# Block products of the feed-forward parts add onto values put into PSUM by ScalarE and VectorE, with one PSUM bank kept for them

## The chip, the cores and the metric

The kernel runs on one core of one Trainium2 chip. The metric is the device time of a run in microseconds (us). The engines are TensorE (PE; its weight loads are shown as PEld), VectorE (DVE), ScalarE (ACT), GpSimd (POOL) and SyncE (SP). PSUM holds what TensorE writes: eight banks, each 128 partitions by 512 float32 values.

## The reference

A causal decoder trunk of two layers on 512 tokens of width 1024 in float32. Layer 0 mixes tokens by dilated attention, layer 1 by causal pooling. A SwiGLU feed-forward part of width 2816 follows each mixer, and this is where the change lies:

```python
def swiglu_ffn(h, w_gate_up, w_down):
    gu = h @ w_gate_up
    gate, up = gu[..., :D_FF], gu[..., D_FF:]
    return (jax.nn.silu(gate) * up) @ w_down

for i in range(DEPTH):
    ...
    x = x + swiglu_ffn(rmsnorm(x, ffn_norm[i]), w_ffn_gate_up[i], w_ffn_down[i])
return rmsnorm(x, final_norm)
```

## The kernel before

Activations lie transposed: chunk `X[k]` holds 128 features by 512 tokens, eight chunks. A float32 operand is split into a rounded part `hi` and a rest `lo` (`split`: one ScalarE copy, L93, and one VectorE subtraction, L96), and a product of two operands takes three matmuls for each chunk of 128: hi·hi, hi·lo, lo·hi.

There are two kinds of products. A plain one (`Product`, L328 to L331) has 512 columns and takes a bank from `ps()`, a pool of eight rotating banks. A block product follows Strassen's scheme with Winograd's sums: two output chunks by two halves of the tokens make a 2 by 2 block matrix, and seven products of 256 columns (`mult`, L461 to L463) replace eight. Each has 4 chunks, so 12 matmuls. `w_pair` and `w_dblock` are the weights for it; `Pair` loads them and forms their sums (L192, L193) and splits, one step at each `pump()`. The sums of the activations are made by `prepare` (for gate and up) and by `operands`, `operands_right` and `operands_left` (for down).

`chained` is the block product of the feed-forward parts. It runs the products "11", "1", "2", "21", "3", "22", "4" in this order, which is also TensorE's order. Three accumulators are used: `alpha` takes "11", and then "2", "3" and "4" on top; ScalarE copies its state to `a`, `b` and `c` ahead of each addition (L537, L545, L553). `gamma` takes "1" (copied to `d`, L541), and "22" on top. `beta` takes "21". VectorE then forms the quarters: `beta + a` (L549), `b - gamma` (L558), `d - c` (L554), and the fourth is the negative of `alpha`.

`strassen_pair` uses `chained` for gate and up of one hidden chunk: two quarters are the gate, which goes through Silu (L1202) and is multiplied onto the other two (L1203, L1204). Each layer has 18 such pairs (chunks 4 to 21; chunks 0 to 3 take plain products). For the down projection hidden chunks 2 to 9 and 10 to 17 form two blocks of four `chained` products each, whose quarters are added to `X` by `down` (L1234). Hidden chunks 0, 1 and 18 to 21 take plain products. Over both layers that is 36 pairs and 16 down blocks, 52 block products.

What the engines do is ordered by a scheduler in the language's layer from the program's order and its priorities. Each engine then runs its own queue in order, and waits on semaphores: counts of what another engine or queue has finished.

Between attention and the first feed-forward part stands `residual(KC - 1, f.p)`: VectorE adds the last attention output product into `X[7]` (L1064). Right behind it `lead = begin(2, 1, range(KC - 1))` starts two plain products of the feed-forward part on the first seven chunks, while the last chunk's scaling and squares are still under way (`note`, L392, L393, L381, L383).

Of the kernel before, what the change touches and what calls it, by code (L numbers as in the profile page):

```python
# [15 lines left out]
P = 128  # L16
# [48 lines left out]
def trunk(ctx: ExitStack, tc: tile.TileContext, xT, xN, norms, w_first, w_qk, w_qkp, w_v0p, w_v12, w_out, w_outp, w_pair, w_down, w_dblock, w_pin, w_pgrp,  # L65
# [16 lines left out]
    def ps():  # L82
        return psum.tile([P, S], F32, tag="ps", name="ps")

# [7 lines left out]
    def split(hi, lo, v, pin=False):  # L92
# [3 lines left out]
        nc.vector.tensor_tensor(lo, v, hi.bitcast(F32), op=OP.subtract)  # L96

    def split_neg(hi, lo, v):
        nc.scalar.activation(hi, v, AF.Copy, scale=-1.0)
        nc.vector.scalar_tensor_tensor(lo, v, -1.0, hi.bitcast(F32), op0=OP.mult, op1=OP.subtract)  # L100

# [198 lines left out]
    class Product:  # L300


        def __init__(self, n, ins, w=None, keep=None):
            self.n, self.ins, self.done, self.p, self.w = n, ins, 0, ps(), w
            self.sizes = units_of(n)
            self.tiles, self.keep = keep or [], keep is not None
# [64 lines left out]
    def stream(layer):  # L371
        return lambda k: operand[layer, k]
# [59 lines left out]

    def begin(n, layer, ks):
        return [Product(KC, stream(layer)).add(ks) for i in range(n)]

# [84 lines left out]

    def chained(T, one, two, scratch, n, inner=False, after={}):
# [12 lines left out]

        wb = part(unit, "b")
        mult(alpha, wb, 0, T, "11", n)
        nc.scalar.copy(a, alpha)  # L537
# [7 lines left out]
        nc.scalar.copy(b, alpha)  # L545
        behind(2)
        mult(beta, wb, 1, T, "21", n)
        wb.done()
        nc.vector.tensor_add(one[:, left], beta, a)  # L549
# [8 lines left out]
        nc.vector.tensor_sub(one[:, right], b, gamma)  # L558
        behind(5)
        w = part(unit, "l")  # L560
        mult(alpha, w, 0, T, "4", n, on=True)
        w.done()
        if not inner:
            nc.scalar.activation(two[:, left], alpha, AF.Copy, scale=-1.0)
        behind(6)
        return alpha

# [37 lines left out]
    with tc.tile_pool(name="opool", bufs=1) as opool:  # L605
        with tc.tile_pool(name="apool", bufs=1) as apool:
# [473 lines left out]
            residual(KC - 1, f.p)  # L1080

    with tc.tile_pool(name="fpool", bufs=2) as fpool:

# [12 lines left out]
        def ffn(layer, nxt, lead, row):  # L1096
# [21 lines left out]
            def prepare(k):  # L1118
# [37 lines left out]
            def operands_right(i, v):  # L1156
                u, t = U["u"], U["t"]
                nc.vector.tensor_sub(t[:, H2:], t[:, :H2], v[:, H2:])
# [6 lines left out]
                nc.vector.tensor_sub(u[:, :H2], v[:, H2:], u[:, H2:])  # L1165
                split(*B["3", i], u[:, :H2])
# [7 lines left out]
            def later(f, *a):  # L1174
                return lambda: f(*a)
# [7 lines left out]

            def strassen_pair(u, first=None, right=None):
# [5 lines left out]
                def act_right():  # L1190
                    nc.scalar.activation(gt[:, H2:], gt[:, H2:], AF.Silu)
                    nc.vector.tensor_mul(u[:, H2:], u[:, H2:], gt[:, H2:])
                    right()

                if first:
                    hooks.setdefault(2, []).extend([later(give, ("t", k, 1)) for k in range(K2)] + [first])
                if right:
                    hooks.setdefault(3, []).append(lambda: nc.scalar.activation(gt[:, :H2], gt[:, :H2], AF.Silu))
                    hooks.setdefault(5, []).append(act_right)
                left = chained(T, gt, u, ftile, K2, inner=True, after=hooks)  # L1200
                if not right:
                    nc.scalar.activation(gt, gt, AF.Silu)  # L1202
                    nc.vector.tensor_mul(u[:, H2:], u[:, H2:], gt[:, H2:])  # L1203
                nc.vector.scalar_tensor_tensor(u[:, :H2], left, -1.0, gt[:, :H2], op0=OP.mult, op1=OP.mult)  # L1204

            def gate_up(j, ahead):
# [3 lines left out]
                if j < NPLAIN:  # L1210
                    plain_pair(j, u)
                elif block and odd and j == FC - 1:
                    strassen_pair(u, later(operands, i, U["even"]), later(operands_right, i, u))
                else:
                    strassen_pair(u)
# [10 lines left out]
                elif not odd:  # L1226
                    U["even"] = u
                elif j == FC - 1:
                    operands_left(i, u)
                else:  # L1230
                    late.extend([later(operands, i, U["even"]), later(operands_right, i, u), later(operands_left, i, u)])
# [7 lines left out]
            for first, end, block in PARTS:  # L1239
# [32 lines left out]

        lead = begin(2, 1, range(KC - 1))
        row = finish(lead, 1, [KC - 1])
# [260 lines left out]
```

## Time and profile before

| what | value |
| --- | --- |
| median of 3 runs | 1184.02 us (1183.59 to 1184.98) |
| profiled execution | 1185.19 us |
| its span, first to last instruction | 1183.4 us |
| mean granted clock of TensorE | 0.999 |
| PE, DVE, ACT, POOL busy | 1173.5, 992.7, 750.4, 174.1 us |

Each row of instructions gives the line, the engine, the operation, the tile written and the tiles read, and a count; then the busy time, the mean duration in ns, and the idle time of the engine just before, with what ended it. `L549` is line 549 of the kernel before, unless the text says that it is one of the changed kernel. `ps` is any PSUM tile of the rotating pool, `near` and `far` hold split operands, `w` and `half` split weights, `raw` loaded weights. A timeline row gives the start, the duration and the instruction.

### The profile page before, as it was taken

What the parts mean: (1) busy time and instruction counts of PE and PEld (TensorE: products, weight loads), DVE (VectorE), ACT (ScalarE), POOL (GpSimd) and SP (SyncE); (2) the same over time, 40 slices, a digit from 0 to 9 for tenths busy, and PEclk for the clock granted to TensorE, in tenths of its full rate; (3) what the DMA queues carried; (4) which work ended last, traced back from release to release, by engine and by line L of the source; (5) the groups of instructions that cost most, each with busy time, mean ns of one, the idle gap of its engine ahead of it and who ended that gap; (6) DMA issues with size and microseconds to landing.
All of it is one profiled execution on the core that took longest, in us unless ns stands there. A gap on an engine that the chain in (4) does not pass through costs nothing.

```text
span 1183.4 us, 25574 instructions
## 1 busy us (share of the span) xinstructions
PE 1173.5 (99%) x10182; PEld 1122.6 (95%) x10182; DVE 992.7 (84%) x1747; ACT 750.4 (63%) x1341; POOL 174.1 (15%) x169
## 2 busy tenths in 40 slices
PE   9999999999999999999999999999999999999997
PEld 7899999999999989889999999988889999999997
DVE  8987898889789988799988988657789988898875
ACT  8764664656556666757756766776575776676553
POOL 2111111211011002301111111112030111111100
PEclk9999999999999999999999999999999999999999
DMA  8757666665766557957777787798595777777732
GB/s 288 166 125 196 166 164 159 172 156 149 187 159 158 153 159 203 244 109 196 192 194 199 190 202 191 201 260 204 117 203 121 190 199 194 191 196 195 188 90 73
DMA packets 85017, 209.97 MB, mean 177 GB/s; under 512 B 7952, under 2 KB 13216, under 8 KB 84896
## 3 DMA queue, kind: packets, MB, share of 16 engines
q1 hardware_dynamic: 53104, 145.63, 37.3%
q0 software_dynamic: 31504, 62.41, 32.6%
q8 instruction: 80, 1.31, 0.4%
q14 instruction: 41, 0.34, 0.1%
q10 hardware_dynamic: 288, 0.29, 0.1%
HBM read 206.19 MB, written 2.10 MB: 176 GB/s over the span
## 4 chain that ended last, share of the span: by engine, by line
PE 97%; issue 1%; ACT 1%; DVE 1%; POOL 0%; DVEq 0%; POOLq 0%; ACTq 0%
PE ps L461 21%; PE ps L463 21%; PE ps L462 21%; PE ps L328 7%; PE ps L331 7%; PE ps L329 7%; PE ps L637 2%; PE ps L852 2%; PE ps L638 2%; PE ps L639 2%; PE ps L943 2%; PE ps L730 1%; PE ps L749 1%; ACT w L93 0%; PE ps L914 0%
## 5 line engine op out<-in xcount | busy, mean ns | idle before, releaser
L93 ACT ACTIVATE w<-raw 128x1024 fp32r<-128x1024 f32 x271 | 286.5, 1062 | 150.3 <-PE ps L463 78.8
L96 DVE TENSOR_TENSOR w<-raw,w 128x1024 fp32r<-128x1024 f32 x271 | 330.6, 1223 | 47.7 <-ACT w L93 43.4
L461 PE MATMUL ps<-far,w 128*128 128x256 f32 x896 | 246.5, 275 | 0.0
L462 PE MATMUL ps<-far,w 128*128 128x256 f32 x896 | 246.5, 275 | 0.0
L463 PE MATMUL ps<-far,w 128*128 128x256 f32 x896 | 246.4, 275 | 0.0
L461 PE MATMUL ps<-near,w 128*128 128x256 f32 x749 | 210.9, 282 | 0.0
L463 PE MATMUL ps<-near,w 128*128 128x256 f32 x749 | 207.1, 276 | 0.0
L462 PE MATMUL ps<-near,w 128*128 128x256 f32 x749 | 207.0, 276 | 0.0
L462 PEld LDWEIGHTS ps<-far,w 128*128 128x128 f32 x896 | 168.2, 188 | 0.1
L461 PEld LDWEIGHTS ps<-far,w 128*128 128x128 f32 x896 | 168.2, 188 | 0.1
L463 PEld LDWEIGHTS ps<-far,w 128*128 128x128 f32 x896 | 168.2, 188 | 0.0
L461 PEld LDWEIGHTS ps<-near,w 128*128 128x128 f32 x749 | 140.7, 188 | 0.5
L462 PEld LDWEIGHTS ps<-near,w 128*128 128x128 f32 x749 | 140.8, 188 | 0.0
L463 PEld LDWEIGHTS ps<-near,w 128*128 128x128 f32 x749 | 140.8, 188 | 0.0
L328 PE MATMUL ps<-near,w 128*128 128x512 f32 (+1 forms) x332 | 125.9, 380 | 0.0
L331 PE MATMUL ps<-near,w 128*128 128x512 f32 (+1 forms) x332 | 125.0, 376 | 0.0
L329 PE MATMUL ps<-near,w 128*128 128x512 f32 (+1 forms) x332 | 124.9, 376 | 0.0
L176 POOL DMA_DIRECT2D raw<-w_pair x36 | 43.6, 1210 | 297.0 <-DMA raw<-w_pair 123.7
L331 PEld LDWEIGHTS ps<-near,w 128*128 128x128 f32 x332 | 62.3, 188 | 11.6
L328 PEld LDWEIGHTS ps<-near,w 128*128 128x128 f32 x332 | 62.3, 188 | 11.5 <-ACT near L93 0.4
L329 PEld LDWEIGHTS ps<-near,w 128*128 128x128 f32 x332 | 62.5, 188 | 11.3 <-DVE near L96 0.2
L192 DVE TENSOR_TENSOR raw<-raw 128x512 f32<-128x512 f32 x87 | 59.7, 686 | 11.5 <-issue 9.7
(342 smaller groups left out, 2730.3 us busy)
## 6 DMA issues: line engine op xcount, KB each, us to landing
raw<-w_pair SPq DMA_DIRECT2D x80, 512.0 KB, 5.1
raw<-w_qkp SPq DMA_DIRECT2D x42, 512.0 KB, 4.6
raw<-w_pair POOLq DMA_DIRECT2D x36, 512.0 KB, 7.6
raw<-w_dblock SPq DMA_DIRECT2D x32, 512.0 KB, 4.5
raw<-w_qkp POOLq DMA_DIRECT2D x21, 512.0 KB, 7.9
rawhalf<-w_pair SPq DMA_DIRECT2D x36, 256.0 KB, 5.3
raw<-w_v SPq DMA_DIRECT2D x16, 512.0 KB, 4.2
raw<-w_dblock POOLq DMA_DIRECT2D x16, 512.0 KB, 7.3
```

The costliest lines, as they stand in the source:

```text
L93: made = nc.scalar.activation(hi, v, AF.Copy)
L96: nc.vector.tensor_tensor(lo, v, hi.bitcast(F32), op=OP.subtract)
L176: nc.gpsimd.dma_start(self.b.rearrange("p (a c) -> p a c", a=2), self.src[:, None, 3 * n:].to_broadcast([P, 2, n]), accum_op=OP.add)
L192: nc.vector.tensor_add(a[:, :n], a[:, :n], b[:, :n])
L328: nc.tensor.matmul(self.p[:, cols], w[0][:, s], mh[:, cols], start=self.done == 0, stop=False)
L329: nc.tensor.matmul(self.p[:, cols], w[0][:, s], ml[:, cols], start=False, stop=False)
L331: nc.tensor.matmul(self.p[:, cols], w[1][:, s], mh[:, cols], start=False, stop=self.done == self.n)
L461: nc.tensor.matmul(dst, w.t[0][:, c], th, start=k == 0 and not on, stop=False, skip_group_check=on)
L462: nc.tensor.matmul(dst, w.t[0][:, c], tl, start=False, stop=False, skip_group_check=on)
L463: nc.tensor.matmul(dst, w.t[1][:, c], th, start=False, stop=k == n - 1, skip_group_check=on)
L637: nc.tensor.matmul(o, mh, wh, start=k == 0, stop=False)
L638: nc.tensor.matmul(o, mh, wl, start=False, stop=False)
```

## The change

The three quarters that VectorE formed after the products are formed by the accumulation in PSUM. After "11" ScalarE writes the copy of alpha into `beta` instead of into `a`, and "21" adds onto it. After "2" VectorE writes `b - d` into `gamma`, and "22", whose operand is no longer negated, adds onto that. The first quarter is then read from `beta`, the third from `gamma`. `split_neg` becomes `split`.

`beta` has a fixed bank of its own, `seeded`. The pool of eight banks is closed after attention, and a pool of seven and the kept bank are opened; the first lead product of layer 0 also goes into the kept bank.

In `strassen_pair` Silu becomes two calls of 256 columns that read `beta` and `gamma` in PSUM. In the down blocks `X[m]` takes two adds of 256 columns from PSUM instead of one of 512 from `one`. The branches that are taken out (`first`, `right`, the deferred `down`) never ran with this kernel's table `PARTS`, whose last part is no block.

```diff
-    psum = ctx.enter_context(tc.tile_pool(name="psum", bufs=8, space=PSUM))
+    first_banks = ExitStack()
+    banks = [first_banks.enter_context(tc.tile_pool(name="psum", bufs=8, space=PSUM))]
...
     def ps():
-        return psum.tile([P, S], F32, tag="ps", name="ps")
+        return banks[-1].tile([P, S], F32, tag="ps", name="ps")
...
-    def begin(n, layer, ks):
-        return [Product(KC, stream(layer)).add(ks) for i in range(n)]
+    def begin(n, layer, ks, p=None):
+        return [Product(KC, stream(layer), p=None if i else p).add(ks) for i in range(n)]
...
-        alpha, beta, gamma = (ps()[:, :H2] for i in range(3))
-        ab, cd = scratch("first"), scratch("sums")
-        a, b, c, d = ab[:, left], ab[:, right], cd[:, left], cd[:, right]
+        alpha, gamma = (ps()[:, :H2] for i in range(2))
+        beta = seeded[0][:, :H2]
+        bs, cd = scratch("first"), scratch("sums")
+        b, c, d = bs[:, left], cd[:, left], cd[:, right]
...
         mult(alpha, wb, 0, T, "11", n)
-        nc.scalar.copy(a, alpha)
+        nc.scalar.copy(beta, alpha)
...
         nc.scalar.copy(b, alpha)
+        nc.vector.tensor_sub(gamma, b, d)
         behind(2)
-        mult(beta, wb, 1, T, "21", n)
+        mult(beta, wb, 1, T, "21", n, on=True)
         wb.done()
-        nc.vector.tensor_add(one[:, left], beta, a)
...
         mult(gamma, wm, 1, T, "22", n, on=True)
         wm.done()
-        nc.vector.tensor_sub(one[:, right], b, gamma)
...
-        return alpha
+        return beta, gamma, alpha
...
+    first_banks.close()
+    banks.append(ctx.enter_context(tc.tile_pool(name="psum7", bufs=7, space=PSUM)))
+    seeded = [ctx.enter_context(tc.tile_pool(name="seeded", bufs=1, space=PSUM)).tile([P, S], F32, tag="seeded", name="seeded")]
...
-                split_neg(*n, b22)
+                split(*n, b22)
...
-                split_neg(*B["22", i], v[:, H2:])
+                split(*B["22", i], v[:, H2:])
...
-                left = chained(T, gt, u, ftile, K2, inner=True, after=hooks)
-                if not right:
-                    nc.scalar.activation(gt, gt, AF.Silu)
-                    nc.vector.tensor_mul(u[:, H2:], u[:, H2:], gt[:, H2:])
+                beta, gamma, left = chained(T, u, ftile, K2, inner=True, after=hooks)
+                nc.scalar.activation(gt[:, :H2], beta, AF.Silu)
+                nc.scalar.activation(gt[:, H2:], gamma, AF.Silu)
+                nc.vector.tensor_mul(u[:, H2:], u[:, H2:], gt[:, H2:])
...
-                        one, two = ftile("one"), ftile("two")
-                        chained(D, one, two, ftile, (end - first) // 2, after=waiting())
-                        for q, v in ((m, one), (m + 1, two)):
-                            if last and m < KC - 2:
-                                late.append(later(down, q, v, last))
-                            else:
-                                down(q, v, last)
+                        two = ftile("two")
+                        parts = chained(D, two, ftile, (end - first) // 2, after=waiting())
+                        for a, p in enumerate(parts[:2]):
+                            x = X[m][:, a * H2:(a + 1) * H2]
+                            nc.vector.tensor_add(x, x, p)
+                        down(m + 1, two, last)
...
-        lead = begin(2, 1, range(KC - 1))
+        lead = begin(2, 1, range(KC - 1), seeded[0])
```

How the order of instructions moves is shown at three places. In each pair of blocks the first is the kernel before and the second the changed one, with its own line numbers. TensorE at the first lead product of layer 0, with the semaphores that each matmul waits for (`DVE_49` counts VectorE's work, `Activation_49` ScalarE's, `DMASW3_49` a DMA queue):

```order
L331 MATMUL ps<-near,w 128x512
L328 MATMUL ps<-near,w 128x512 [waits Activation_49]
L329 MATMUL ps<-near,w 128x512
L331 MATMUL ps<-near,w 128x512 [waits DMASW3_49]
L328 MATMUL ps<-near,w 128x512
```

```order
L328 MATMUL ps<-near,w 128x512
L325 MATMUL seeded<-near,w 128x512 [waits DVE_49,Activation_49]
L326 MATMUL seeded<-near,w 128x512
L328 MATMUL seeded<-near,w 128x512 [waits DMASW3_49]
L325 MATMUL seeded<-near,w 128x512
```

The first lead product (`seeded<-near,w`) waits for VectorE as well; the count in the built program is that of the residual add L1064 of `X[7]` (L1061 of the changed kernel).

VectorE in a gate/up pair of layer 1 in which operands of the down projection are also made (the pair that starts at 940.8 us; `gt` is the gate, `first` and `sums` hold `a` to `d`):

```order
L1165 TENSOR_TENSOR u<-u 128x256
L96 TENSOR_TENSOR near<-t,near 128x256
L96 TENSOR_TENSOR near<-u,near 128x256 x2
L1171 SCALAR_TENSOR_TENSOR u<-t,u 128x256
L549 TENSOR_TENSOR gt<-ps,first 128x256
L96 TENSOR_TENSOR w<-raw,w 128x1024
L554 TENSOR_TENSOR u<-sums 128x256
L96 TENSOR_TENSOR near<-u,near 128x256
L96 TENSOR_TENSOR w<-raw,w 128x1024
L558 TENSOR_TENSOR gt<-first,ps 128x256
```

```order
L1166 TENSOR_TENSOR u<-u 128x256
L97 TENSOR_TENSOR near<-t,near 128x256
L97 TENSOR_TENSOR near<-u,near 128x256
L544 TENSOR_TENSOR ps<-first,sums 128x256
L97 TENSOR_TENSOR near<-u,near 128x256
L1172 SCALAR_TENSOR_TENSOR u<-t,u 128x256
L97 TENSOR_TENSOR w<-raw,w 128x1024
L552 TENSOR_TENSOR u<-sums 128x256
L97 TENSOR_TENSOR near<-u,near 128x256
L97 TENSOR_TENSOR w<-raw,w 128x1024 x2
```

L549 and L558 are gone, and the seed of gamma (L544) stands two operand instructions ahead of where L549 stood.

ScalarE in the same pair (`sums<-ps` is `d` or `c`, `first<-ps` is `a` or `b`):

```order
L545 COPY first<-ps 128x256
L93 ACTIVATE near<-u 128x256
L93 ACTIVATE w<-raw 128x1024
L93 ACTIVATE near<-u 128x256
L553 COPY sums<-ps 128x256
L93 ACTIVATE w<-raw 128x1024 x2
L93 ACTIVATE half<-rawhalf 128x512
L1202 ACTIVATE gt<-gt 128x512
L537 COPY first<-ps 128x256
```

```order
L543 COPY first<-ps 128x256
L94 ACTIVATE near<-u 128x256
L94 ACTIVATE w<-raw 128x1024
L94 ACTIVATE near<-u 128x256
L1191 ACTIVATE gt<-seeded 128x256
L551 COPY sums<-ps 128x256
L94 ACTIVATE w<-raw 128x1024 x2
L1192 ACTIVATE gt<-ps 128x256
L94 ACTIVATE half<-rawhalf 128x512
L535 COPY seeded<-ps 128x256
```

The first half of Silu (L1191) moves ahead of the copy of `c`, the second (L1192) behind the two weight splits; the copy that made `a` now writes `seeded`. In the down blocks VectorE's add of `beta` into `X` stands right behind the seed of gamma.

More of the change, by code (lines that the diff above doesn't have):

```diff
@@ L300, in trunk, with __init__ @@
     class Product:
[L303 to L304 removed]
+        def __init__(self, n, ins, w=None, keep=None, p=None):
+            self.n, self.ins, self.done, self.p, self.w = n, ins, 0, ps() if p is None else p, w
             self.sizes = units_of(n)
@@ L519, in seven, with chained @@
         behind(6)
-    def chained(T, one, two, scratch, n, inner=False, after={}):
+    def chained(T, two, scratch, n, inner=False, after={}):
         (unit,), = units.popleft()
         left, right = slice(0, H2), slice(H2, S)
-        alpha, beta, gamma = (ps()[:, :H2] for i in range(3))
-        ab, cd = scratch("first"), scratch("sums")
-        a, b, c, d = ab[:, left], ab[:, right], cd[:, left], cd[:, right]
+        alpha, gamma = (ps()[:, :H2] for i in range(2))
+        beta = seeded[0][:, :H2]
+        bs, cd = scratch("first"), scratch("sums")
+        b, c, d = bs[:, left], cd[:, left], cd[:, right]
         def behind(i):
@@ L1182, in waiting, with strassen_pair @@
                 return hooks
-            def strassen_pair(u, first=None, right=None):
+            def strassen_pair(u):
                 gt = ftile("gt")
@@ L1188, in strassen_pair @@
                     hooks.setdefault(1, []).append(later(keep, *U.pop("keep")))
-                def act_right():
-                    nc.scalar.activation(gt[:, H2:], gt[:, H2:], AF.Silu)
-                    nc.vector.tensor_mul(u[:, H2:], u[:, H2:], gt[:, H2:])
[L1193 to L1199, printed above, removed]
-                left = chained(T, gt, u, ftile, K2, inner=True, after=hooks)
-                if not right:
-                    nc.scalar.activation(gt, gt, AF.Silu)
-                    nc.vector.tensor_mul(u[:, H2:], u[:, H2:], gt[:, H2:])
+                beta, gamma, left = chained(T, u, ftile, K2, inner=True, after=hooks)
+                nc.scalar.activation(gt[:, :H2], beta, AF.Silu)
+                nc.scalar.activation(gt[:, H2:], gamma, AF.Silu)
+                nc.vector.tensor_mul(u[:, H2:], u[:, H2:], gt[:, H2:])
                 nc.vector.scalar_tensor_tensor(u[:, :H2], left, -1.0, gt[:, :H2], op0=OP.mult, op1=OP.mult)
@@ L1211, in gate_up @@
                     plain_pair(j, u)
-                elif block and odd and j == FC - 1:
-                    strassen_pair(u, later(operands, i, U["even"]), later(operands_right, i, u))
                 else:
```

5 lines of the change are left out of this document (removed).

## Prediction

> **What bounds the kernel now.** I read the page's busy times and chain first, then the waits of TensorE alone, then stretches of the feed-forward parts, then single instructions at the places that the change touches. From the page, busy time and the head of the chain that ended last:
>
> ```profile
> PE 1173.5 (99%) x10182; PEld 1122.6 (95%) x10182; DVE 992.7 (84%) x1747; ACT 750.4 (63%) x1341; POOL 174.1 (15%) x169
> ...
> PE 97%; issue 1%; ACT 1%; DVE 1%; POOL 0%; DVEq 0%; POOLq 0%; ACTq 0%
> ```
>
> TensorE (PE) is 97% of the chain. Its spans are modelled, so I ask what it waited for, and count its matmuls in four stretches that hold block products (us, busy and count of each engine, granted clock, DMA):
>
> ```profile
> PE ps L914 <- DVE idle L911: 1.2, 1, 1.2
> PE ps L780 <- PE ps L463: 0.5, 1, 0.5
> PE ps L780 <- DVE far L768: 0.3, 1, 0.3
> ...
> 521.00:616.00 95.00, 95.00 (x840) 95.00 (x839) 84.11 (x148) 64.59 (x112) 11.01 (x10) 1.00 0.70 182
> 616.00:759.00 143.00, 143.00 (x1265) 143.00 (x1264) 124.87 (x211) 94.98 (x167) 16.84 (x14) 1.00 0.74 190
> 902.00:998.00 96.00, 96.00 (x845) 95.88 (x844) 85.12 (x150) 65.10 (x113) 11.52 (x10) 1.00 0.71 181
> 998.00:1150.00 152.00, 152.00 (x1343) 152.00 (x1342) 131.04 (x219) 99.89 (x173) 16.34 (x14) 1.00 0.69 178
> ```
>
> TensorE's waits come to 2.0 us in all, and all lie before the feed-forward parts (L911, L768 and L780 are attention code). In the stretches one matmul of 256 columns starts every 113 ns: 95/840 = 0.1131, 143/1265 = 0.1130, 96/845 = 0.1136, 152/1343 = 0.1132. VectorE (DVE) is busy for 86 to 89% of them and nothing of that reaches TensorE. So a product of 12 matmuls takes 1.36 us, and a block product of seven 9.5 us. The change leaves these counts alone: it can gain only what TensorE waits for, which here is nothing, and it can lose wherever it makes TensorE wait.
>
> **The change part by part.** First what it takes off VectorE and ScalarE (ACT). Groups by line and shape (count | busy us, mean ns | idle before):
>
> ```profile
> L549 DVE TENSOR_TENSOR gt<-ps,first 128x256 f32<-128x256 f32 x36 | 15.2, 422 | 10.2 <-PE ps L463 10.2
> L558 DVE TENSOR_TENSOR gt<-first,ps 128x256 f32<-128x256 f32 x36 | 15.0, 415 | 0.1
> L516 DVE TENSOR_TENSOR ps<-ps,sums 128x512 f32<-128x512 f32 x21 | 14.6, 693 | 0.0
> L1234 DVE TENSOR_TENSOR x<-x,two 128x512 f32<-128x512 f32 x16 | 11.0, 686 | 0.0
> L1234 DVE TENSOR_TENSOR x<-x,one 128x512 f32<-128x512 f32 x16 | 11.0, 686 | 0.0
> L537 ACT COPY first<-ps 128x256 f32<-128x256 f32 x52 | 19.4, 373 | 14.9 <-PE ps L463 14.7
> L564 ACT ACTIVATE two<-ps 128x256 f32<-128x256 f32 x16 | 6.2, 385 | 4.2 <-PE ps L463 4.2
> L93 ACT ACTIVATE near<-u 128x256 fp32r<-128x256 f32 x48 | 19.9, 415 | 8.0 <-DVE u L1204 6.9 <-DVE u L1165 0.6 <-DVE u L1171 0.5
> L1202 ACT ACTIVATE gt<-gt 128x512 f32<-128x512 f32 x36 | 22.2, 618 | 2.2 <-DVE gt L558 2.2
> L1158 DVE TENSOR_TENSOR t<-t,u 128x256 f32<-128x256 f32 x16 | 6.7, 421 | 0.0
> ```
>
> VectorE: each of the 36 gate/up pairs loses L549 and L558 (837 ns) and gains the seed of gamma (L544 of the changed kernel). The one VectorE row that writes PSUM is L516, 693 ns for 512 columns against 686 for L1234, which writes SBUF, so I take the seed at 0.42 us, bounded by half of 693 and by 693. That is 0.42 us less, 15 us over 36 pairs. Each of the 16 down blocks loses L549, L558 and the 686 ns add of `one`, and gains the seed and two adds of 256 columns from PSUM at about 422 ns each: 0.26 us less, 4 us. The new signs (L96 for L100, a plain split for a negated one) are the same instructions within some ns. These 19 us of VectorE time buy nothing: TensorE waited for none of them, above.
>
> ScalarE: the copy that made `a` (L537, 373 ns) now writes `seeded`. No row shows ScalarE writing PSUM; the nearest are 373 ns (from PSUM) and 415 (SBUF to SBUF), and I take 373 with 415 as the dear end. Silu was one call of 618 ns on 512 columns from SBUF and becomes two of 256 from PSUM, each like L564: 2 x 385 - 618 = 0.15 us more in each of 36 pairs, 5.5 us. ScalarE is 63% busy, so what counts is only whether a copy becomes late.
>
> [...]
>
> **Deadlines in the tightest pair.** TensorE runs "11", "1", "2", "21", "3", "22", "4". New is that "22" waits for the seed of gamma, which needs `b`, copied after "2"; "21" needs the seed of beta, which stands where the copy of `a` stood, and "2" had to wait for that copy already. The pair that starts at 940.8 us has the shortest slack in the trace (start us, us, instruction):
>
> ```profile
> 945.58 0.35 ACT L545 COPY first<-ps 128x256 f32<-128x256 f32 x1
> 946.24 0.28 PE L461 MATMUL ps<-far,w 128*128 128x256 f32 x1
> ...
> 945.81 0.42 DVE L96 TENSOR_TENSOR near<-t,near 128x256 fp32r<-128x256 f32 x1
> 946.14 0.76 DVE L96 TENSOR_TENSOR near<-u,near 128x256 fp32r<-128x256 f32 x2
> 946.81 0.42 DVE L1171 SCALAR_TENSOR_TENSOR u<-t,u 128x256 f32<-128x256 f32 x1
> 947.15 0.42 DVE L549 TENSOR_TENSOR gt<-ps,first 128x256 f32<-128x256 f32 x1
> 947.60 0.28 PE L461 MATMUL ps<-far,w 128*128 128x256 f32 x1
> ```
>
> The row at 946.24 opens "3", the one at 947.60 "22". L549 ended at 947.57, just ahead of "22", but the new order puts the seed ahead of the last L96 and of L1171, so it starts near 946.48 and ends near 946.90, 0.7 us early. Behind it VectorE goes on at once. I cost it at 0. If the seed took twice 0.42 us it would still fit; at 1.1 us it would not.
>
> The copy of `b` ended at 945.93, 0.31 us before "3" needs alpha. The 0.15 us more of Silu can come out of that slack and leaves 0.16 us; the handover of a finished ScalarE write to a waiting matmul took 0.06 us (772.90 to 772.96 in the rows below). So 0 again, but this is the thin place. Sixteen pairs carry such operand work (L1158, x16).
>
> At the end of the first layer the seed has less: its copy ends at 761.58 and "2" starts at 761.72. At the dear end (+0.04) it still fits.
>
> ```profile
> 761.23 0.35 ACT L537 COPY first<-ps 128x256 f32<-128x256 f32 x1
> 761.72 0.30 PE L461 MATMUL ps<-far,w 128*128 128x256 f32 x1
> ```
>
> **Last pair of layer 0.** Here Silu, two VectorE products and a split of `up` stand between the pair and the last chunk that the first down product reads:
>
> ```profile
> 770.83 0.62 ACT L1202 ACTIVATE gt<-gt 128x512 f32<-128x512 f32 x1
> ...
> 772.27 0.63 ACT L93 ACTIVATE near<-up 128x512 fp32r<-128x512 f32 x1 [0.30 <-DVE up L1204]
> ...
> 772.58 0.39 PE L331 MATMUL ps<-near,w 128*128 128x512 f32 x1
> 772.96 0.50 PE L328 MATMUL ps<-near,w 128*128 128x512 f32 x1
> ```
>
> The step from 772.58 to 772.96 is 0.38 us where its neighbours take 0.23, so this chain is already late, and the 0.15 us of the second Silu may come on top; in part it overlaps VectorE's work. I take 0.1 us, between 0 and 0.15.
>
> **The switch of PSUM pools.** This is the term that decides. The eight-bank pool is closed after attention, and the first lead product of layer 0 goes into `seeded`. In the order its first matmul now also waits for VectorE; the count it waits for is that of L1064, the last residual add, which reads the product just before it from another bank. Before, that matmul waited only for its weights. Rows there:
>
> ```profile
> 465.49 0.69 DVE L383 TENSOR_TENSOR sq<-sq 128x512 f32<-128x512 f32 x1
> 466.09 0.68 DVE L1064 TENSOR_TENSOR x<-x,ps 128x512 f32<-128x512 f32 x1
> ...
> 469.03 0.69 DVE L383 TENSOR_TENSOR sq<-sq 128x512 f32<-128x512 f32 x1 [0.71 <-ACT sq L381]
> ...
> 464.81 0.39 PE L331 MATMUL ps<-near,w 128*128 128x512 f32 x1
> 465.04 0.39 PE L328 MATMUL ps<-near,w 128*128 128x512 f32 x1
> ```
>
> 464.81 is the last matmul of the attention output, 465.04 the first of the lead. L1064 ends at 466.09 + 0.68 = 466.77; VectorE's order up to there is unchanged. With 0.06 us of handover the lead starts at 466.83 instead of 465.04: 1.79 us. Queued behind that matmul on TensorE is everything that follows, and since TensorE waits for nothing later up to the tail, nothing gives the time back: ScalarE, VectorE and the weight loads only run further ahead. Ends of this term: 0 if the wait is over in time, 469.72 - 465.04 = 4.7 us if TensorE had to wait for the whole norm work of that chunk (second L383). I take 1.79, which the waited count names.
>
> **Seven banks.** A block product takes two rotating banks instead of three, so they come round later, and elsewhere a product takes one bank; a seventh instead of an eighth product back is 7 x 5.5 us in the pooling part (24 matmuls at 0.23). Cost 0.
>
> **Sum.** 1.79 + 0.1 + 0 = 1.9 us. The profiled execution took 1185.19 us for a span of 1183.4; it becomes 1187.1. That execution lies 1.17 above the median of the runs, 1184.02, so the forecast is 1184.02 + 1.9 = 1185.9 us, 0.16% slower. A difference under 0.2%, 2.4 us, is about what a measurement of this kernel cannot tell from no change; the forecast lies just inside.
>
> **The rivals.**
> - ScalarE becomes the bound in the block products (slower). Place: the copy of `b` in the 16 pairs with operand work, with 0.16 us left less 0.06 of handover. From 0.1 us more on (dearer Silu or seed) TensorE waits in each: 0.2 us over the point costs 16 x 0.2 = 3.2 us, 1189.1. For it: the copy waits behind splits that wait for VectorE. Against: VectorE runs 0.42 us lighter in every pair, which brings those splits forward. Chance 0.15.
> - The wait at the switch is covered, so the change does nothing to the time: 1184.1. For it: only if VectorE reaches L1064 earlier; it has no idle time just ahead of it, so little speaks for it. Chance 0.1.
> - The one kept bank serialises the block products: the next seed must wait for the readers of beta (Silu, or the add into X), and if a reader ran as late as L1202 does it would end 0.3 us ahead of the seed. A reader 1 us later than that would make TensorE wait in all 52 products, 5.2 us for each 0.1 us: 1189 and up. Against: the order puts both readers right after the seed of gamma or ahead of the copy of `c`, about half a block product earlier. Chance 0.04. [...]
> - Less traffic from VectorE lets matmuls start faster than 113 ns (faster): 4368 matmuls x 1 ns = 4.4 us, 1181.5. Against: the four stretches differ in VectorE's share from 0.86 to 0.89 and not in the step. Chance 0.06.
>
> **How the numbers follow.** Forecast 0.65, with its own range 1185.2 to 1187.0 (the last-pair term 0 to 0.15, ScalarE's thin place up to half a us, half a us between medians of runs). About 0.17 of it lies above 1186.4 and counts as slower. Slower: 0.17 + 0.15 + 0.04 = 0.36. Within 0.2%: 0.48 + 0.1 = 0.58. Faster 0.06. For 8 in 10 I leave out the gain, the kept bank and the upper half of the ScalarE rival: 1184.0 to 1188.4.
>
> **What would show it.** Right: TensorE idle for about 1.8 us between L328 matmuls near 465 us, ended by the residual add; block products at 113 ns a matmul; VectorE's busy time down by 19 us, ScalarE's up by some 5. Wrong: no such gap, waits of TensorE for ScalarE or VectorE inside the block products, or another matmul step.

## The result, and the profile after

| kernel | median, us | range, us | ratio to before, 95% interval |
| --- | --- | --- | --- |
| before (16 runs) | 1183.82 | 1183.17 to 1187.51 | |
| changed (16 runs) | 1186.55 | 1185.29 to 1190.21 | 1.0027 [1.0018, 1.0036] |

The medians lie 2.7 us apart (1186.55 − 1183.82), 0.23%; the ratio, 1.0027, is taken over all runs and not from the medians, so the long ones count in it. The change makes the kernel slower. The profiled execution of the changed kernel took 1189.34 us, one of the long ones: five of the 16 runs lie between 1188.9 and 1190.3 us with a mean granted clock of 0.995 to 0.997, ten between 1185.2 and 1186.9 (1186.39 in the middle) with 0.997 to 0.999, and one at 1188.12 with 0.999. Line numbers are now those of the changed kernel unless another is named.

The page's busy times, then TensorE's waits (total, times, longest, us), then the four stretches of the feed-forward parts, 4 us later than the ones shown of before, because everything there runs 4 us later:

```profile
PE 1174.0 (99%) x10182; PEld 1122.6 (95%) x10182; DVE 978.4 (82%) x1711; ACT 747.7 (63%) x1377; POOL 174.3 (15%) x169
```

```profile
PE seeded L325 <- DVE x L1061: 3.0, 1, 3.0
PE ps L911 <- DVE idle L908: 1.2, 1, 1.2
PE ps L777 <- PE ps L460: 0.9, 1, 0.9
```

```profile
525.00:620.00 95.00, 95.00 (x839) 94.96 (x838) 81.74 (x142) 63.68 (x119) 10.89 (x9) 1.00 0.71 182
620.00:763.00 143.00, 143.00 (x1264) 143.00 (x1264) 120.24 (x200) 94.32 (x176) 16.97 (x14) 1.00 0.73 190
906.00:1002.00 96.00, 96.00 (x845) 95.84 (x845) 82.75 (x144) 64.31 (x120) 10.91 (x9) 1.00 0.72 181
1002.00:1154.00 152.00, 152.00 (x1344) 152.00 (x1343) 126.49 (x209) 99.17 (x185) 16.94 (x14) 1.00 0.71 179
```

VectorE lost 14.3 us of busy time (992.7 to 978.4) and nothing came of it: the step of a 256-column matmul is what it was, 95/839 = 0.1132, 143/1264 = 0.1131, 96/845 = 0.1136, 152/1344 = 0.1131 us. The one large new row is the first: the lead matmul waits 3.0 us for the last residual add. Before, this row did not exist.

TensorE there (start, duration, instruction, idle before), the change's largest effect in one view:

```profile
464.12 0.39 PE L328 MATMUL ps<-near,w 128*128 128x512 f32 x1
467.48 0.47 PE L325 MATMUL seeded<-near,w 128*128 128x512 f32 x1 [2.97 <-DVE x L1061]
...
468.25 0.43 PE L325 MATMUL seeded<-near,w 128*128 128x512 f32 x1
468.49 0.62 PE L326 MATMUL seeded<-near,w 128*128 128x512 f32 x1
468.90 0.63 PE L328 MATMUL seeded<-near,w 128*128 128x512 f32 x1
...
471.46 0.60 PE L328 MATMUL seeded<-near,w 128*128 128x512 f32 x1
471.89 0.40 PE L325 MATMUL seeded<-near,w 128*128 128x512 f32 x1
```

Two losses follow each other. First, idle time from 464.51 to 467.48. Then, from 468.49 on, a matmul of 512 columns starts every 0.42 to 0.43 us where its neighbours take 0.23: eight stretched steps, 3.40 us in place of 1.81, that cost 1.6 us together. The granted clock says what that is (windows; after the busy times comes PEclk, the granted clock):

```profile
467.50:468.49 0.99, 0.99 (x5) 0.81 (x6) 0.37 (x1) 0.99 (x2) 0.00 (x0) 1.00 1.06 257
468.49:471.90 3.41, 3.41 (x10) 2.64 (x9) 1.08 (x2) 1.07 (x2) 0.88 (x1) 0.50 1.06 256
471.90:475.00 3.10, 3.10 (x15) 2.55 (x14) 0.00 (x0) 0.00 (x0) 0.00 (x0) 1.00 1.13 272
```

For 3.41 us TensorE had half its clock. Matched matmul by matmul, this execution ran 0.7 us ahead of the profiled one of before when it reached the switch, 2.4 us behind at the lead, 4.1 us behind after the stretch at half rate, and still 4.1 us behind at TensorE's last matmul. So the wait cost 3.1 us (2.97 of idle time and a handover), nothing is lost in the block products, and nothing is given back.

Why 3.0 us and not the 1.8 forecast stands in VectorE's and ScalarE's rows ahead of that residual add:

```profile
462.55 0.69 DVE L97 TENSOR_TENSOR half<-rawhalf,half 128x512 fp32r<-128x512 f32 x1 [0.20 <-ACT half L94]
464.11 0.75 DVE L390 SCALAR_TENSOR_TENSOR near<-x,nrm,near 128x512 fp32r<-128x512 f32 x1 [0.87 <-ACT near L389]
...
466.64 0.69 DVE L1061 TENSOR_TENSOR x<-x,ps 128x512 f32<-128x512 f32 x1
```

```profile
460.93 1.06 ACT L146 ACTIVATE w<-raw 128x1024 fp32r<-128x1024 f32 x1 [1.33 <-DMA raw<-w_pair]
461.90 0.62 ACT L94 ACTIVATE half<-rawhalf 128x512 fp32r<-128x512 f32 x1
...
463.37 0.71 ACT L389 ACTIVATE near<-x,nrm 128x512 fp32r<-128x512 f32 x1
```

ScalarE stood 1.33 us for a weight load (DMA). Behind that weight split, in the same queue, stands L389, which scales a chunk; VectorE's L390 needs it; and two L390 with their squares stand ahead of L1061. So VectorE stood 0.20 and 0.87 us there, the residual add ended at 467.33, and TensorE went on 0.15 us later. The 1.8 us of the forecast and these 1.07 make 2.9 of the 3.0. In the profile of before ScalarE took that weight (L149) without such a wait, and VectorE had no idle time there:

```profile
460.20 1.04 ACT L149 ACTIVATE w<-raw 128x1024 fp32r<-128x1024 f32 x1
```

### The profile page after: what moved, and what is told of

Same layout as the page of the kernel before. It is cut to its first block, busy times and chain, and to the rows that moved or that the text cites. A ratio compares the mean times of both kernels' runs of the same rounds, so it can differ in the third digit from the quotient of the medians.

```text
span 1186.8 us, 25576 instructions
## 1 busy us (share of the span) xinstructions
PE 1174.0 (99%) x10182; PEld 1122.6 (95%) x10182; DVE 978.4 (82%) x1711; ACT 747.7 (63%) x1377; POOL 174.3 (15%) x169
## 4 chain that ended last, share of the span: by engine, by line
PE 95%; issue 1%; DVE 1%; DMA 1%; ACT 1%; SPq 0%; POOL 0%; DVEq 0%; POOLq 0%; ACTq 0%
PE ps L458 19%; PE ps L460 19%; PE ps L459 19%; PE ps L325 6%; PE ps L326 6%; PE ps L328 6%; PE ps L849 2%; PE ps L634 2%; PE ps L635 2%; PE ps L636 2%; PE seeded L460 2%; PE seeded L459 2%; PE seeded L458 2%; PE ps L940 2%; PE ps L727 1%
## 5 line engine op out<-in xcount | busy, mean ns | idle before, releaser
L459 PE MATMUL ps<-far,w 128*128 128x256 f32 x736 | 202.4, 275 | 0.0
L458 PE MATMUL ps<-far,w 128*128 128x256 f32 x736 | 202.4, 275 | 0.0
L460 PE MATMUL ps<-far,w 128*128 128x256 f32 x736 | 202.4, 275 | 0.0
L458 PE MATMUL ps<-near,w 128*128 128x256 f32 x701 | 197.7, 282 | 0.0
L460 PE MATMUL ps<-near,w 128*128 128x256 f32 x701 | 193.8, 277 | 0.0
L459 PE MATMUL ps<-near,w 128*128 128x256 f32 x701 | 193.8, 277 | 0.0
L459 PEld LDWEIGHTS ps<-far,w 128*128 128x128 f32 x736 | 138.2, 188 | 0.1
L458 PEld LDWEIGHTS ps<-far,w 128*128 128x128 f32 x736 | 138.2, 188 | 0.1
L460 PEld LDWEIGHTS ps<-far,w 128*128 128x128 f32 x736 | 138.2, 188 | 0.0
L458 PEld LDWEIGHTS ps<-near,w 128*128 128x128 f32 x701 | 131.7, 188 | 0.5
L459 PEld LDWEIGHTS ps<-near,w 128*128 128x128 f32 x701 | 131.8, 188 | 0.0
L460 PEld LDWEIGHTS ps<-near,w 128*128 128x128 f32 x701 | 131.8, 188 | 0.0
L325 PE MATMUL ps<-near,w 128*128 128x512 f32 (+1 forms) x324 | 122.8, 380 | 0.0
L326 PE MATMUL ps<-near,w 128*128 128x512 f32 (+1 forms) x324 | 121.9, 376 | 0.0
L328 PE MATMUL ps<-near,w 128*128 128x512 f32 (+1 forms) x324 | 121.8, 376 | 0.0
L326 PEld LDWEIGHTS ps<-near,w 128*128 128x128 f32 x324 | 61.0, 188 | 11.3 <-DVE near L97 0.4
L328 PEld LDWEIGHTS ps<-near,w 128*128 128x128 f32 x324 | 60.8, 188 | 11.2
L325 PEld LDWEIGHTS ps<-near,w 128*128 128x128 f32 x324 | 60.8, 188 | 11.1 <-ACT near L94 0.2
```

The lines of the kernel that those rows point to most:

```text
L325: nc.tensor.matmul(self.p[:, cols], w[0][:, s], mh[:, cols], start=self.done == 0, stop=False)
L326: nc.tensor.matmul(self.p[:, cols], w[0][:, s], ml[:, cols], start=False, stop=False)
L328: nc.tensor.matmul(self.p[:, cols], w[1][:, s], mh[:, cols], start=False, stop=self.done == self.n)
L458: nc.tensor.matmul(dst, w.t[0][:, c], th, start=k == 0 and not on, stop=False, skip_group_check=on)
L459: nc.tensor.matmul(dst, w.t[0][:, c], tl, start=False, stop=False, skip_group_check=on)
L460: nc.tensor.matmul(dst, w.t[1][:, c], th, start=False, stop=k == n - 1, skip_group_check=on)
```

## The experiments

Two explanations were to be told apart. **Theory A**: the block products cost nothing, and all of the loss comes from closing the pool: the first matmul into a newly opened bank waits until the last reader of the closed pool is through, wherever that reader stands in its engine's queue, with a stretch at half rate on top in some executions, like the 3.41 us in the profile after. **The rivals**: ScalarE (or the kept bank) has become a bound in the block products, or the switch has a price of its own.

**The change without the switch.** One pool of eight banks for the whole kernel; the kept bank is its first tile taken after attention, so that seven rotate.

```diff
-    first_banks = ExitStack()
-    banks = [first_banks.enter_context(tc.tile_pool(name="psum", bufs=8, space=PSUM))]
+    banks = [ctx.enter_context(tc.tile_pool(name="psum", bufs=8, space=PSUM))]
...
-    first_banks.close()
-    banks.append(ctx.enter_context(tc.tile_pool(name="psum7", bufs=7, space=PSUM)))
-    seeded = [ctx.enter_context(tc.tile_pool(name="seeded", bufs=1, space=PSUM)).tile([P, S], F32, tag="seeded", name="seeded")]
+    seeded = [ps()]
```

> The changed kernel, but the pool of eight banks stays open and the kept bank is one of its tiles, taken once ahead of the feed-forward parts; nothing else differs. Theory A (the whole loss is made at the switch of pools): TensorE does not wait near 465 us and runs on at full clock there; the time is that of the kernel before, ratio 0.9995 to 1.0005. Rival B (part of the loss is in the block products, through ScalarE's copies or the second Silu call): TensorE waits or steps over 113 ns in the stretches 521 to 759 and 902 to 1150 us, and 1 to 2 us of the loss stay, ratio 1.001 or more. Rival C (less work on VectorE gains something that the switch hid): ratio under 0.999.

Measured: 1184.45 us (1183.71 to 1188.5, 11 runs), ratio 1.0005 [0.9997, 1.0014]. TensorE's waits in its profile, where no row of a lead matmul is left:

```profile
PE ps L910 <- DVE idle L907: 1.2, 1, 1.2
PE ps L776 <- PE ps L459: 0.6, 1, 0.6
PE ps L776 <- DVE far L764: 0.3, 1, 0.3
```

The new block products with one kept bank and seven rotating ones take the time of the old ones: of the 4366 steps from one of their matmuls to the next, one is longer than 0.15 us, as in the profile of before. This rules out the kept bank, the seven banks and ScalarE as causes of the 2.7 us.

**The switch without the change.** The kernel before, whose pool of eight banks is closed at the same place and opened again with eight.

```diff
...
+    first_banks.close()
+    banks.append(ctx.enter_context(tc.tile_pool(name="psum2", bufs=8, space=PSUM)))
```

> The kernel before with the switch alone: its pool of eight banks is closed after attention and a new one of eight is opened; block products, Silu and VectorE's sums are as before. Theory A: the first lead matmul waits for the last residual add, 1.8 us where ScalarE is not held up by a weight load just ahead and about 3 us where it is, and in the long case some 8 matmuls of 512 columns follow at 427 ns instead of 227; median 2.5 to 4 us over before, ratio 1.002 to 1.0035, like the changed kernel. Rival B: about half of that, ratio 1.001.

Measured: 1187.06 us (1185.67 to 1190.1, 11 runs), ratio 1.0025 [1.0016, 1.0034]: the whole loss of the change, with none of its block products. The wait, and ScalarE's hold-up ahead of it:

```profile
PE ps L329 <- DVE x L1065: 3.3, 1, 3.3
```

```profile
462.23 1.07 ACT L150 ACTIVATE w<-raw 128x1024 fp32r<-128x1024 f32 x1 [1.68 <-DMA raw<-w_pair]
```

VectorE stood 0.56 and 0.87 us behind it, so here 1.8 and 1.43 make 3.2 of the 3.3 us. No matmul behind the wait ran at half rate in this profiled execution, whose granted clock is 1.00 from 465.50 to 476.00 us; but four of the 11 runs have a mean clock of 0.997 or less, and they are the four longest, 1188.77 to 1190.1.

**A longer wait.** Two VectorE adds ahead of the last residual add of the changed kernel.

```diff
+            for i in range(2):
+                nc.vector.tensor_add(one, f.p, two)
             residual(KC - 1, f.p)
```

> The changed kernel with two more VectorE adds of 512 columns between the last attention product and its residual add, each some 0.6 us, so that the wait at the switch is longer by 1.2 us in every run. Theory A with a clock that falls after a long wait: wait 3.0 to 4.3 us, followed in nearly every run by about 8 matmuls at half rate (1.6 us); median 4.5 to 6 us over before, ratio 1.004 to 1.005, in one group instead of two. Rival D (the half-rate stretch of the profiled run was an accident that has nothing to do with the wait's length): the wait alone grows, median 1.2 us over the changed kernel, 3.7 over before, ratio 1.0031.

Measured: 1187.88 us (1187.33 to 1189.19, 5 runs), ratio 1.0035 [1.0022, 1.0048], 1.3 us above the changed kernel. The wait in the profiled execution was 3.1 us, no longer than in the profile without the adds, and seven matmul steps were stretched, five of them to 0.42 or 0.43 us:

```profile
PE seeded L325 <- DVE x L1061: 3.1, 1, 3.1
```

But this wait is made up otherwise. ScalarE took its weight without standing for it, and the two adds stand in VectorE's queue, 1.31 us from the first one's start to that of the residual add:

```profile
460.00 1.04 ACT L146 ACTIVATE w<-raw 128x1024 fp32r<-128x1024 f32 x1
```

```profile
465.95 1.40 DVE L1078 TENSOR_TENSOR one<-ps,one 128x512 f32<-128x512 f32 x2
467.26 0.68 DVE L1061 TENSOR_TENSOR x<-x,ps 128x512 f32<-128x512 f32 x1
```

The wait of 3.10 us less 1.31 is 1.79 us, what the prediction took for a switch without a late load.

One run of the five, the profiled one, has a mean clock of 0.997, and three have 0.999, so a stretch at half rate in nearly every run, which I had expected under theory A, missed. Between profiles a late load changes the wait by about as much as this dose.

**ScalarE's copy twice.** The kernel without the switch, with ScalarE's seed written twice in each of the 52 block products.

```diff
         nc.scalar.copy(beta, alpha)
+        nc.scalar.copy(beta, alpha)
```

> As the run with the kept bank taken from the open pool, but the copy of alpha into beta is made twice in each block product, 0.28 us of ScalarE more. The forecast's thin place (0.16 us left at the copy of b in the pairs with operand work, less a handover of 0.06) says: those pairs and their neighbours, 16 to 30 of 52, now make TensorE wait 0.1 to 0.25 us each, 3 to 6 us over before, ratio 1.0025 to 1.005. Rival (ScalarE has more room than the rows suggest): no wait, ratio 1.000.

Measured: 1194.32 us (1193.97 to 1195.15, 4 runs), ratio 1.0088 [1.0074, 1.0102], 9.9 us above the kernel without the switch: more than the 3 to 6 us expected. One of the places, where "2" opens, on TensorE and on ScalarE:

```profile
581.18 0.28 PE L459 MATMUL ps<-far,w 128*128 128x256 f32 x1
581.51 0.38 PE L457 MATMUL ps<-far,w 128*128 128x256 f32 x1
581.73 0.28 PE L458 MATMUL ps<-far,w 128*128 128x256 f32 x1
```

```profile
580.47 0.37 ACT L534 COPY ps<-ps 128x256 f32<-128x256 f32 x1
580.77 0.41 ACT L93 ACTIVATE near<-u 128x256 fp32r<-128x256 f32 x1
581.09 0.37 ACT L535 COPY ps<-ps 128x256 f32<-128x256 f32 x1
```

The second copy ends at 581.46 and "2" starts at 581.51, 0.33 us after the matmul ahead of it instead of 0.11, and the step behind it takes 0.22. In 27 of the 52 block products these two steps are stretched, by 0.22 to 0.33 us together; over all block products the steps sum to 9.3 us above 113.4 ns each, their mean in the kernel without the switch. So ScalarE does come to bound these products with 0.37 us more; by these rows it has, as an estimate, only 0.04 to 0.15 us to spare in half of them (0.37 less 0.33 and 0.22). With the copy once, it has just enough.

**VectorE's seed twice.** The same, for VectorE's write of gamma.

```diff
         nc.vector.tensor_sub(gamma, b, d)
+        nc.vector.tensor_sub(gamma, b, d)
```

> The held-bank kernel (one pool of eight banks, one of them kept from the start, no switch), with VectorE's seed of gamma written twice in each of the 52 block products: 0.42 us more of VectorE time each, 22 us in all. Theory (prediction: VectorE has about 0.7 us to spare ahead of "22", and its spans of idle time take the rest): as the held-bank kernel, 1184.45 us, ratio 0.9997 to 1.0014. Rival (VectorE's margin is as thin as ScalarE's turned out to be): 0.2 to 0.3 us of wait in half of the block products, 5 to 8 us, ratio 1.004 to 1.007.

Measured: 1185.69 us (1184.93 to 1186.52, 11 runs), ratio 1.001 [1.0001, 1.0018], 1.2 us above the median of the kernel without the switch. The intervals of the two ratios overlap, so from the times alone it is not clear that the 22 us of VectorE time cost anything; the profile shows about 1 us. In it 11 steps between matmuls of block products are 0.05 to 0.11 us longer than 113 ns, 1.0 us together (in the profile of the kernel without the switch there is one). One of them, right behind the first matmul of "3", and under it the copy of `b` on ScalarE:

```profile
573.23 0.28 PE L459 MATMUL ps<-far,w 128*128 128x256 f32 x1
573.35 0.37 PE L457 MATMUL ps<-far,w 128*128 128x256 f32 x1
573.56 0.28 PE L458 MATMUL ps<-far,w 128*128 128x256 f32 x1
```

```profile
572.93 0.35 ACT L542 COPY first<-ps 128x256 f32<-128x256 f32 x1
```

The copy ended at 573.28 there, just ahead of the matmul at 573.35. Ten of the 11 steps stand behind the first matmul of "3". It is the place that the prediction called thin; "22", which the doubled write delays directly, has no stretched step.

**The residual add earlier in VectorE's queue.** The changed kernel; `note` of chunks 5 and 6 stands in the program behind the last residual add.

```diff
-            def residual(m, p):
+            def residual(m, p, noted=True):
...
-                note(1, m)
+                if noted:
+                    note(1, m)
...
-                    residual(NOUT + 2 * u + c, p)
+                    residual(NOUT + 2 * u + c, p, not u)
...
-            residual(KC - 1, f.p)
+            residual(KC - 1, f.p, False)
+            for m in range(KC - 3, KC):
+                note(1, m)
```

> The changed kernel, with the scaling and squares of chunks 5 and 6 (note) moved in the program behind the last residual add. In VectorE's order two L390 (0.67 us apart from their neighbours each) then stand behind the add into X[7] instead of ahead of it, so it ends about 1.4 us earlier. Theory A (the switch costs what the first lead matmul waits for the last reader of the closed pool, wherever that stands in VectorE's queue): the wait of 3.0 us becomes about 1.6 us, no stretch at half rate, 1184.45 + 1.6 = 1186.0 us or less, ratio to before 1.0008 to 1.0015. Rival S (the price belongs to the switch itself, closing and opening pools, or to VectorE's use of the kept bank): wait and time as in the changed kernel, 1186.5 us, ratio 1.0025 or more.

Measured: 1185.11 us (1184.51 to 1188.57, 11 runs), ratio 1.0013 [1.0004, 1.0022]. The wait in the profiled execution:

```profile
PE seeded L325 <- DVE x L1061: 0.9, 1, 0.9
```

Here VectorE stood ready at the residual add and the 0.9 us are that add itself, behind the attention product. The profiled execution was a long one (1188.57 us): TensorE had lost 2.4 and 1.6 us in attention, which gave the other engines time, so 0.9 us is the short end. The times do not rest on it: of the 0.27% half is gone by reordering VectorE's and ScalarE's work alone, with the switch in place, and 0.13% is what theory A expected. A price of the switch itself would have stayed.

**The switch one product earlier.** The changed kernel, with the three lines of the switch ahead of `f = Product(HEADS, heads)`.

```diff
+            first_banks.close()
...
             f = Product(HEADS, heads).add(range(HEADS))
...
-    first_banks.close()
```

> The changed kernel, with the pools switched one product earlier, ahead of the last attention output product. Its first matmul then waits for VectorE's last sum of the block product before it (L513), which ended at 460.31 us where that matmul started at 458.85 us in the changed kernel's trace. Theory A: a wait of 1.5 to 1.7 us ended by that sum stands at 459 us, none at the lead product near 465 us, and no stretch at half rate; 1184.45 + 1.6 = 1186.0 us, ratio 1.0010 to 1.0018. Rival S (the price belongs to the kept bank and the lead product): wait still at the lead product, 1186.5 us, ratio 1.0025 or more.

Measured: 1185.86 us (1185.45 to 1186.55, 11 runs), ratio 1.0014 [1.0005, 1.0023]. The wait was 1.4 us for the 1.5 to 1.7 expected:

```profile
PE ps L325 <- DVE one L513: 1.4, 1, 1.4
```

The wait moved with the switch, to a matmul that writes `ps` and not the kept bank, and is ended by the last reader there. It does not hang on the lead product or on `seeded`. No run has a mean clock below 0.998, and the times lie within 1.1 us.

**Six adds.** The dose of two adds raised to six.

```diff
+            for i in range(6):
+                nc.vector.tensor_add(one, f.p, two)
             residual(KC - 1, f.p)
```

> The changed kernel, with six more VectorE adds of 512 columns (0.6 us each from start to start) ahead of the last residual add: that add ends about 3.6 us later, counted from the 1.8 us of wait that VectorE's queue gives without a late weight load. Theory A: a wait of 5.3 to 5.5 us. [...] Rival (the half-rate stretch has nothing to do with the length of the wait and comes in some runs only): median 1189.9 us, ratio 1.0042 to 1.0050.

Measured: 1193.21 us (1192.52 to 1194.05, 5 runs), ratio 1.0074 [1.0059, 1.0088]. The wait, and the granted clock in two windows:

```profile
PE seeded L325 <- DVE x L1061: 6.8, 1, 6.8
```

```profile
465.97:469.38 3.41, 0.00 (x0) 0.00 (x0) 3.27 (x6) 1.31 (x2) 0.86 (x1) 1.00 1.07 265
469.38:476.20 6.82, 4.96 (x12) 3.97 (x13) 3.04 (x5) 1.24 (x2) 0.57 (x1) 0.50 1.10 258
```

The wait came out larger (6.8 us for 5.4): the six adds took 0.72 us each and not 0.60 from start to start, and ScalarE was again held up by a weight load, by 0.98 us, which gave VectorE 0.79 us of idle time. The stretch at half rate cost 2.3 us. What was to be decided is whether the half rate comes in some runs only, as the rival has it with a median of 1189.9 us, or in every run of this kernel; the 1.6 us of the profile after in every run would give 1184.45 (the median without the switch) + 5.4 + 1.6 = 1191.4 us, an estimate. The time lies above both, and all five runs have a mean clock of 0.995 or 0.996. By this sign the half rate is in every run of this kernel, in some runs of the kernels whose profiles have waits of 3.0 to 3.3 us, and in none of the 11 runs each of the two kernels above, whose profiles have waits of 1.4 and 0.9 us. It is a sign and no proof: the mean also holds the end of the program, where the clock is at 0.50 for the last 2.5 us in the profile of before and for the last 4.9 in that of the changed kernel, and one of the 27 runs of before that were timed with these kernels has 0.997 too.

## Why the prediction was right or wrong

The time, 1185.9 us, was 0.65 us short of the median, inside the range; the side and the place were right. But 0.58 of the chances stood on a difference within 0.2%, and the ratio came out at 1.0027. That the median lies so near is in part luck: it falls among the short runs, ten of 16, while the mean of all 16, 1187.44 us, is 3.25 us above that of before (1184.19), where the sum had 1.9. Point by point, by its own steps:

- **Nothing to gain in the block products: right.** The step of 113 ns stayed, and the kernel without the switch ties with before, 1.0005 [0.9997, 1.0014]. That VectorE's relief would speed up matmuls is refuted by the same two numbers.
- **VectorE 19 us less, ScalarE some 5 more: right as sums of durations** (all instructions of each engine added up, VectorE 18.8 us less, ScalarE 5.6 us more), while the busy times of the page, which count overlapping instructions once, moved by −14.3 and −2.7. The new rows (count | busy us, mean ns | idle before):

```profile
L544 DVE TENSOR_TENSOR ps<-first,sums 128x256 f32<-128x256 f32 x52 | 22.4, 431 | 15.2 <-ACT first L543 15.0
L535 ACT COPY seeded<-ps 128x256 f32<-128x256 f32 x52 | 18.7, 360 | 22.3 <-PE ps L460 22.0
L1192 ACT ACTIVATE gt<-ps 128x256 f32<-128x256 f32 x36 | 13.4, 372 | 0.0
L1191 ACT ACTIVATE gt<-seeded 128x256 f32<-128x256 f32 x36 | 13.1, 364 | 0.0
```

  The seed by VectorE took 431 ns (420 taken), ScalarE's 360 (between 373 and 415 taken: it was cheaper than either end), a Silu half 364 to 372 (385 taken).
- **ScalarE's thin place: right that it holds, and right that it is thin.** Doubling VectorE's seed used it up. Doubling ScalarE's copy showed that the copy ahead of "2" is as thin, and in half of the block products: I had shown 0.14 us of room there for one pair (761.58 to 761.72) and costed it at nothing because "2" had to wait for that copy before.
- **The last pair of layer 0, 0.1 us: measured 0.04.** The long steps there took 0.379 and 0.341 us before, and now 0.277, 0.392 and 0.338; the changed execution was 4.07 us behind ahead of them and 4.11 us behind after them.
- **Seven banks and the kept bank, 0: right.** The kept bank is in use too, only outside the rotation, and the kernel without the switch loses nothing by it, the ratio above; so this case shows that seven rotating banks are enough here, not that a bank can be spared.
- **The switch, 1.79 us: the mechanism and the place were right, the size was not.** This is the step that failed. I took the end of the residual add from the profile of before, "VectorE's order up to there is unchanged". The order was; the times were not. TensorE had not waited for that add before, so one execution in which ScalarE got its weight in time told nothing of how late it can be. In the profiles of the changed kernel, of the switch alone and of the six adds ScalarE stood 1.33, 1.68 and 0.98 us for a weight load just ahead, and the waits were 3.0 and 3.3 us (and 6.8 with the adds). Where the load came in time, in the profile with two adds, the wait less the adds was the 1.79 us that I took. The handover took 0.15 us and not 0.06. And the stretch at half rate, 1.6 us in the profiled execution, had no term at all. The upper end of the term, 4.7 us, happens to be about what wait and stretch cost together in that execution (3.1 and 1.6), but for another reason.

That the late weight load is what lengthens the wait is read from three profiles with it and one, with two adds, without it; the reordered kernel, where the add no longer stands behind the scaled chunks, agrees. No experiment moved the load by itself, and why it comes late in some executions is open. The long runs of the changed kernel lie 3 us above the others. A late load and the half rate together would give 1.2 + 1.6 = 2.8 us, an estimate from the profiles (3.0 less 1.8, and the stretch); that both fall into the same runs is not shown, as only the profiled executions show their waits.

## What to carry to other kernels

Closing a PSUM pool in the middle of the program was a barrier for TensorE here: the first matmul into the new pool waited for the last reader of the old one, 3.0 us in the changed kernel, 3.3 with the switch alone, 1.4 with the switch one product earlier. So the switch belongs where that reader is done early, or is avoided by keeping a bank out of the one pool (here the ratio falls from 1.0027 to 1.0005). When a change makes an engine wait for something that nobody waited for before, its time in one old profile is not its price: follow that instruction's own queue upstream to whatever can be late, here a weight load that ScalarE stood for by up to 1.68 us, and put that into the range. And work taken off an engine that nobody waits for bought nothing here: 19 us of VectorE time, at a ratio of 1.0005 without the switch.

## What the hardware showed unexpectedly

In the middle of a dense program TensorE's granted clock fell to 0.50 at waits of 3.0 to 6.8 us. In the changed kernel it fell at 468.49 us, one microsecond after the matmuls had begun again, for 3.41 us; with two adds at 467.52, 0.56 us before they began again, for 3.41 us too; and with six adds at 469.38, in the middle of the 6.8 us wait, for 6.82 us, twice that. 512 columns then took 427 ns from start to start instead of 227 (in the changed kernel 468.90 to 471.46 us for six of them, and 463.21 to 464.12 for four).

The 3.3 us wait of the switch alone was spared. The run with two adds ahead of the fall and behind it, and under it the switch alone in its wait and behind it:

```profile
464.50:467.50 3.00, 0.48 (x3) 0.06 (x1) 2.97 (x6) 2.39 (x3) 0.14 (x1) 1.00 1.11 286
467.52:470.93 3.41, 2.85 (x7) 2.29 (x8) 1.77 (x3) 1.24 (x2) 1.47 (x2) 0.50 1.07 247
...
465.50:468.70 3.20, 0.00 (x0) 0.00 (x0) 3.12 (x5) 2.52 (x5) 1.95 (x3) 1.00 1.08 273
468.70:472.20 3.50, 3.44 (x15) 2.87 (x16) 1.44 (x2) 2.14 (x3) 0.88 (x1) 1.00 1.07 265
```

With two adds the clock fell after 2.5 us of idle time, and in the switch alone it stayed at 1.00 through 3.2 us without a matmul and the 3.5 us behind them. So the length of the wait does not decide alone, and by the sign of the mean clocks one kernel pays for it in some executions and not in others: the five longest runs of the changed kernel have 0.995 to 0.997, ten of the other eleven 0.998 or 0.999. Nor does the clock fall at a fixed time after the idle time begins: it fell after 4.0 us in the changed kernel, 2.5 with two adds and 5.0 with six. At the end of the program it fell 1.8 us after the last matmul in the changed kernel and 4.9 in the kernel before. What decides is not shown, and these numbers give no general limit.
